# One-core block pair in f32: T by transposes, the last product with tokens on partitions, gathered modulation planned behind the norm, half-wide attention results in the last layer

## The chip, the cores and the metric

The kernel runs on one NeuronCore of a Trainium2 chip. The time is the device time of one execution in microseconds (us). Engines are written as in the profile: PE (TensorE matmul), PEld (TensorE weight load), DVE (VectorE), ACT (ScalarE), POOL (GpSimd), SP (SyncE, which issues all DMAs here).

## The reference

Two blocks in sequence on 256 tokens of width D = 1024, in f32. The first block has two layers, each of them a gated FFN, an attention mix and a second gated FFN; the second block has three mixers (RWKV-7, latent attention, differential attention), a gated merge, and an FFN with a short convolution. Cut to what the change touches:

```python
# first block, per layer l; x and a context of 256 tokens, each with its own modulation
mod = silu(c) @ w_ada[l] + b_ada[l]            # 9 vectors of width D: shift, scale, gate, three times
h = h + 0.5 * g1 * swiglu(modulate(rms_norm(h, norm_ffn1[l]), sh1, sc1), w_gate, w_up, w_down)   # FF = 2816
h = h + gm * (concat(y_w, y_g, y_n) @ w_out[l])         # attention; the context too, except in the last layer
h = h + 0.5 * g2 * swiglu(modulate(rms_norm(h, norm_ffn2[l]), sh2, sc2), ...)

# second block: the state of RWKV-7, token by token
sa = einsum('bhij,bhj->bhi', state, -kk_t)
state = state * w_t + sa[..., None] * b_t + v_t[..., None] * k_t

# its last product, and the final norm
u = conv3(rmsnorm(x, norm_ffn) @ w_up) + conv_b
x = x + (silu(gate) * val) @ w_down            # [256, 2816] @ [2816, 1024]
return rmsnorm(x, norm_final)
```

## The kernel before

**Precision.** An f32 product is made of three fp32r matmuls: each operand is split into a high and a low part (hi·hi, hi·lo, lo·hi). Every weight tile arrives by DMA in one of three slots "w"; ACT casts the high part to a "page" and DVE subtracts it from the tile for the low part (`TENSOR_TENSOR page<-w,page`). Activations lie with features on partitions and tokens along the row: 256 columns, or 512 where the context goes along.

**The order of the work.** Every operation is recorded first (`Plan`), and a list scheduler of the kernel's own then sets one fixed order per engine under limits on memory; `nc.after(i, j)` makes operation i wait for operation j in that planning. All instructions are issued from one line, L740 (L741 in the changed kernel). Memory is cut into pages of 2048 words per partition, a "small" area, three weight slots "w" and eight PSUM "banks"; one page can hold several tiles.

**Modulation.** `ada_steps(l, m)` gathers the modulation vector m of layer l: w_ada comes in row blocks `araw` of 128x1024, and each is multiplied by a column of silu(c) and added to `aacc`, for the tokens and for the context (r). That is 14 DVE operations of 128x1024 and two ACT copies for each m. They are recorded as "fill" steps between the tiles of the FFNs by `pop_fill`. Layer 0's m = 0 and 1 are made in another way (`first_mod`), inside the first FFN's first product: for each of eight k, DVE makes the modulation of 128 features (`mod0`, `G00`), scales the input and splits it, and PE then runs 12 matmuls 128x512 on it.

**T.** `rwkv_chunks` treats RWKV-7 in chunks of 128 tokens. For each of four (q, tb), with four heads in one 128x512 tile, the inverse of a triangular matrix is built level by level: W from X (eight matmuls that write 128x128, four of them pairs), a masked copy Wt by DVE, then

```python
pz = Wt^T Z ; px = Z^T Wt ; X -= px ; Z -= pz        # four 128x128 f32 matmuls each, one DVE 128x512 each
```

X is the transpose of Z throughout. Of five levels the last makes only Z, so px is made in 16 levels in all. The two tb of a q run interleaved.

**The last product.** `conv_ffn` loops over eight output blocks o; each takes two weight tiles of 1408 columns (`w2_dn`) and 22 x 3 matmuls 128x256 into one bank, DVE adds the result to the residual `hx`, and `norm_add` squares it for the sum over features. After the last block PE sums and broadcasts the norm, DVE scales eight blocks (`fin`), and eight DMAs of 128 KB write the result.

## Time and profile before

| what | value |
|---|---|
| time, median of 3 runs | 2346.76 us (2346.3 to 2348.51) |
| profiled execution | 2345.4 us, span 2343.5 us |
| mean granted TensorE clock | 0.990 of full speed |
| instructions | 35351 |
| busy share of the span | PE 98%, PEld 85%, DVE 70%, ACT 43%, POOL 2% |
| DMA | 328.20 MB, mean 140 GB/s |

The span runs from the first to the last instruction, and the 1.9 us between it and the execution's own time lie around it. PE is nearly always busy, so a microsecond that leaves PE's own work, or a stall of PE, is what can show in the time; work of DVE or ACT shows only where PE waits for it.

### The profile page before, as it was taken

The page shows a single profiled execution, that of the slowest core. Times are in us where ns is not written, and L with a number is a line of the kernel's source. Part 1 is how long each engine was busy: PE and PEld are TensorE (multiplying, and loading weights), DVE is VectorE, ACT ScalarE, POOL GpSimd, SP SyncE. Part 2 cuts the span into 40 slices and gives each one's busy share as a digit, 9 for nine tenths or more (in the row PEclk, how much of TensorE's full clock was granted, in tenths as well). Part 3 has the DMA queues.
Part 4 walks back from the last instruction along what each step waited for, and adds up shares of the span by engine and source line. Part 5 has one row for each costly group of instructions (what it writes and reads, how often), then busy time and mean ns, then how long its engine had stood idle before and what let it go on. Part 6 is the DMA issues. An engine that isn't in the chain of part 4 may idle for free. (4 is left out here: it accounts for less than half of the span.)

```text
span 2343.5 us, 35351 instructions
## 1 busy us (share of the span) xinstructions
PE 2288.6 (98%) x14170; PEld 2003.4 (85%) x14170; DVE 1632.0 (70%) x2860; ACT 1005.9 (43%) x1785; POOL 52.8 (2%) x66
## 2 busy tenths in 40 slices
PE   7999999999999999999999999999999999999998
PEld 5777788978787788788878888789999998999998
DVE  6948763795779999995333348776567767658874
ACT  3422322585543233233222236665456224646653
POOL 0000000010000000000000000000000010000000
PEclk9999999999999999999999999999999999999999
DMA  8636633203136775223132232234544111454543
GB/s 345 229 115 219 236 109 116 82 28 119 62 126 232 243 276 174 83 103 135 51 125 103 68 106 98 86 104 173 197 162 172 42 55 46 153 180 162 198 163 126
DMA packets 63106, 328.20 MB, mean 140 GB/s; under 512 B 8029, under 2 KB 11101, under 8 KB 40030
## 3 DMA queue, kind: packets, MB, share of 16 engines
q1 hardware_dynamic: 62942, 325.95, 39.3%
q8 instruction: 111, 1.82, 0.3%
q14 instruction: 53, 0.43, 0.1%
HBM read 324.87 MB, written 1.05 MB: 139 GB/s over the span
## 5 line engine op out<-in xcount | busy, mean ns | idle before, releaser
L740 PE MATMUL bank<-page,page 128*128 128x256 f32 (+8 forms) x12548 | 2163.4, 334 | 22.4 <-ACT page L740 14.6
L740 PEld LDWEIGHTS bank<-page,page 128*128 128x128 f32 (+3 forms) x12548 | 1846.6, 189 | 277.4 <-ACT page L740 34.8
L740 ACT CAST page<-w 128x1024 fp32r<-128x1024 f32 (+2 forms) x511 | 489.4, 962 | 898.3 <-PE bank L740 866.5
L740 DVE TENSOR_TENSOR page<-w,page 128x1024 fp32r<-128x1024 f32 (+2 forms) x511 | 566.3, 1112 | 375.6 <-ACT page L740 255.6
L740 DVE SCALAR_TENSOR_TENSOR page<-page,page,page 128x1024 f32<-128x1024 f32 x200 | 247.1, 1277 | 1.0 <-ACT page L740 1.0
L740 DVE TENSOR_TENSOR page<-page,bank 128x512 f32<-128x512 f32 (+2 forms) x168 | 93.7, 574 | 135.5 <-PE bank L740 132.9
L740 DVE SCALAR_TENSOR_TENSOR page<-bank,small,page 128x256 f32<-128x256 f32 (+2 forms) x240 | 111.4, 483 | 58.3 <-PE bank L740 55.4
L740 PE MATMUL bank<-page 128*128 128x256 f32 (+7 forms) x650 | 151.8, 308 | 0.0
L740 ACT ACTIVATE page<-bank,small 128x256 f32<-128x256 f32 (+2 forms) x216 | 115.3, 546 | 35.8 <-DVE small L740 25.8
L740 PE MATMUL bank<-small,page 128*128 128x128 f32 (+2 forms) x776 | 110.8, 270 | 19.4 <-DVE page L740 14.2
L740 PEld LDWEIGHTS bank<-small,page 128*128 128x128 f32 x776 | 95.3, 164 | 36.5 <-issue 13.1
L740 DVE TENSOR_TENSOR page<-page,page 128x256 fp32r<-128x256 f32 (+4 forms) x227 | 111.9, 507 | 12.7 <-ACT page L740 11.8
L740 ACT COPY page<-bank 128x512 f32<-128x512 f32 (+3 forms) x175 | 80.8, 496 | 85.2 <-PE bank L740 79.7
L740 ACT CAST page<-page 128x256 fp32r<-128x256 f32 (+1 forms) x165 | 78.0, 484 | 91.5 <-DVE page L740 89.3
L740 ACT ACTIVATE page<-bank 128x512 f32<-128x512 f32 (+3 forms) x163 | 81.7, 508 | 72.7 <-PE bank L740 72.0
L740 PEld LDWEIGHTS bank<-page 128*128 128x128 f32 (+2 forms) x650 | 105.1, 189 | 6.0 <-issue 0.7
L740 ACT ACTIVATE page<-page 128x256 f32<-128x256 f32 (+4 forms) x182 | 80.0, 454 | 57.9 <-DVE page L740 50.9
L740 ACT ACTIVATE page<-page,small 128x256 fp32r<-128x256 f32 (+1 forms) x124 | 56.9, 506 | 52.6 <-DVE page L740 26.0
L740 POOL TENSOR_TENSOR small<-small 128x2 f32<-128x2 f32 (+2 forms) x32 | 38.6, 1207 | 1793.5 <-DVE small L740 1453.1
L740 DVE TENSOR_TENSOR page<-bank,page 128x256 f32<-128x256 f32 (+2 forms) x109 | 51.6, 497 | 34.8 <-ACT page L740 19.7
L740 DVE TENSOR_REDUCE small<-bank 128x1 f32<-128x512 f32 (+3 forms) x132 | 67.3, 527 | 7.1 <-PE bank L740 6.8
L740 DVE COPY_PREDICATED page<-page,small 128x384 f32<-128x384 uint32 x124 | 66.2, 592 | 0.8
(51 smaller groups left out, 580.1 us busy)
## 6 DMA issues: line engine op xcount, KB each, us to landing
w<-in_gu_dram SPq DMA_DIRECT2D x88, 1024.0 KB, 4.8
page<-in_w_ada_dram SPq DMA_DIRECT2D x128, 512.0 KB, 4.6
w<-in_dn_dram SPq DMA_DIRECT2D x64, 704.0 KB, 4.0
w<-in_w_up_dram SPq DMA_DIRECT2D x22, 1024.0 KB, 4.8
w<-in_w_qk_dram SPq DMA_DIRECT2D x12, 1024.0 KB, 4.9
w<-in_w_gate_dram SPq DMA_DIRECT2D x12, 1024.0 KB, 4.8
w<-in_w_dn_dram SPq DMA_DIRECT2D x16, 704.0 KB, 4.0
page<-in_w_ada_dram SPq DMA_DIRECT2D x8, 1024.0 KB, 15.1
```

The source lines that it names most:

```text
L740: getattr(getattr(self.real, eng), m_)(*a_, **k_)
```

## The change

Four edits.

1. **T by transposes.** px and `X -= px` go. Z is updated first, and X is made from it by four PE transposes into one bank and one ACT copy 128x512 (`transposed`), in each of the 16 levels.
2. **The last product with tokens on partitions.** H is the stationary operand now (128 tokens) and the weights move, 512 columns at a time: 22 f x 2 tb x 2 column halves x 3 matmuls 128x512 into four banks that are held throughout; eleven weight tiles of 2048 columns. The residual is transposed beforehand (16 PE transposes, four ACT copies). The final norm is per partition: DVE add, ACT square with a row sum, DVE, POOL power, DVE scale by `gain_out`, and four output DMAs of 256 KB.
3. **Gathered modulation planned behind the norm.** The planner's mark, which was set by each `pop_fill`, is set once in `ffn`: behind the first product (first FFN of layer 0) or behind the norm. Layer 0's m = 2 and layer 1's m = 0 wait for it.
4. **y half wide.** The attention results of the last layer take 256 columns in place of 512 (there is no context there), which frees memory.

```diff
@@ pop_fill / ada_steps / ffn @@
         if self.fill:
-            self.mark = len(self.nc.ops) - 1
             self.fill.pop(0)()
...
-                        if l and m == 0:
+                        if m == (0 if l else 2):
                             nc.after(i, self.mark)
...
+            u_end = len(nc.ops) - 1
             for j in range(ahead):
                 glu(j, first[j], both[0])
-                self.pop_fill()
...
             u = self.norm(l, i_n, halves, rb if one else None)
+        self.mark = u_end if raws else len(nc.ops) - 1
...
-        y = [self.blk(f"y{j}") for j in range(KB)]
+        y = [self.blk(f"y{j}", S if last else T2) for j in range(KB)]
@@ rwkv_chunks @@
+        def transposed(z, x):
+            ps = hv(self.aux_ps("XT"))
+            with nc.run():
+                for hl in range(4):
+                    nc.tensor.transpose(ps[:, hl], z[:, hl], self.ident)
+            nc.scalar.copy(x, ps)
...
+                nc.vector.tensor_tensor(Z, Z, pz, op=OP.subtract)
                 if lv < 4:
-                    px = hv(self.aux_ps("px"))
-                    for hl in range(4):
-                        nc.tensor.matmul(px[:, hl], Z[:, hl], W[:, hl], start=True, stop=True)
-                    nc.vector.tensor_tensor(X, X, px, op=OP.subtract)
-                nc.vector.tensor_tensor(Z, Z, pz, op=OP.subtract)
+                    transposed(Z, X)
@@ conv_ffn @@
-        for o in range(KB):
-            ps = self.mm_ps("pdn")[:, :S]
-            for half in range(2):
-                w = self.wtile(a["w2_dn"][2 * o + half])
-                self.dense(ps, w, 0, H[HFB * half:], nk=HFB, first=half == 0, last=half == 1)
-            nc.vector.tensor_tensor(self.hx[:, o], self.hx[:, o], ps, op=OP.add)
-            self.norm_add(0, o)
-        rb = self.norm_rb(0)
-        for k in range(KB):
-            t = self.t256("fin")
-            nc.vector.scalar_tensor_tensor(t, self.hx[:, k], col[:, 74 + k:75 + k], rb, op0=OP.mult, op1=OP.mult)
-            nc.sync.dma_start(self.out[:, k], t)
+        gain = self.load("gain_out", [D])
...
+        pss = [[self.aux_ps("pdn") for _ in range(2)] for _ in range(2)]
+        def down(f, w, tb):
+            for c in range(2):
+                self.mm3n(pss[tb][c], w, D * (f % 2) + 512 * c, 512, H[f], slice(P * tb, P * tb + P),
+                          f == 0, f == NFB - 1)
...
+        for tb in range(2):
+            st = self.t("fst", [4])
+            for c in range(2):
+                x = xt[tb][:, 512 * c:512 * c + 512]
+                nc.vector.tensor_tensor(x, x, pss[tb][c], op=OP.add)
+                sq = self.t("fsq", [512])
+                nc.scalar.activation(sq, x, AF.Square, scale=1.0 / 32, accum_out=st[:, c:c + 1])
+            nc.vector.tensor_scalar(st[:, 2:3], st[:, 0:1], st[:, 1:2], EPS, op0=OP.add, op1=OP.add)
+            nc.gpsimd.tensor_tensor(st[:, 3:4], st[:, 2:3], self.mhalf[:, :1], op=OP.pow)
+            for c in range(2):
+                cs = slice(512 * c, 512 * c + 512)
+                o = self.t("fin", [512])
+                nc.vector.scalar_tensor_tensor(o, xt[tb][:, cs], st[:, 3:4], gain[:, cs], op0=OP.mult, op1=OP.mult)
+                nc.sync.dma_start(self.out[P * tb:P * tb + P, cs], o)
```

The planner sets the order anew, so instructions move on every engine. Three places follow.

**DVE in the first FFN's first product, near its end.** `SCALAR_TENSOR_TENSOR page,page,page 128x1024` are the accumulations of layer 0's m = 2; the 128x2 rows are modulation and `G00`, `TENSOR_SCALAR 128x256` scales the input, and the `TENSOR_TENSOR 128x256` after it is its low part, for which PE waits. Before:

```order
L740 SCALAR_TENSOR_TENSOR small<-small 128x2
L740 SCALAR_TENSOR_TENSOR page_106<-page_128,page_75,page_106 128x1024
L740 TENSOR_SCALAR page_75<-page_75,small 128x256
L740 SCALAR_TENSOR_TENSOR page_106<-page_128,page_75,page_106 128x1024
L740 TENSOR_TENSOR page_363<-page_75,page_363 128x256
L740 TENSOR_TENSOR page_363<-page_88,page_363 128x256
L740 TENSOR_TENSOR small<-bank_73,small 128x2
L740 SCALAR_TENSOR_TENSOR page_106<-page_135,page_75,page_106 128x1024
L740 TENSOR_TENSOR small<-bank_73,small 128x2
L740 SCALAR_TENSOR_TENSOR page_106<-page_135,page_75,page_106 128x1024
L740 SCALAR_TENSOR_TENSOR small<-small 128x2
L740 SCALAR_TENSOR_TENSOR page_106<-page_135,page_75,page_106 128x1024
```

And now, from the same instruction on:

```order
L741 SCALAR_TENSOR_TENSOR small<-small 128x2
L741 TENSOR_SCALAR page_75<-page_75,small 128x256
L741 TENSOR_TENSOR page_363<-page_75,page_363 128x256
L741 TENSOR_TENSOR page_363<-page_88,page_363 128x256
L741 TENSOR_TENSOR small<-bank_73,small 128x2 x2
L741 SCALAR_TENSOR_TENSOR small<-small 128x2
L741 TENSOR_SCALAR page_75<-page_75,small 128x256
L741 TENSOR_TENSOR small<-bank_67,small 128x2 x2
L741 TENSOR_TENSOR page_420<-page_75,page_420 128x256
L741 TENSOR_TENSOR page_420<-page_88,page_420 128x256
```

The accumulations have left this stretch; the first now stands 18 rows further on, behind the last split of the input and the low parts of the next weight tile.

**PE in the first half of T.** The rows 128x128 x4 with two pages are pz or px (before), the pairs x2 are W. Rows `bank<-small,page 128x128 x4` are four transposes (the identity lies in "small"). 128x256 rows are products of the mixers' input, which fill between. Before, one level of one chunk and the next of the other:

```order
L740 MATMUL bank_70<-page_10668,page_13579 128x128 x4
L740 MATMUL bank_73<-page_13579,page_10668 128x128 x4
L740 MATMUL bank_72<-page_13526,page_13636 128x128 x4
L740 MATMUL bank_71<-page_13636,page_13526 128x128 x3
L740 MATMUL bank_73<-page_13526,page_10668 128x128 x2
L740 MATMUL bank_73<-page_13526,page_1454 128x128 x2
```

And now:

```order
L741 MATMUL bank_68<-page_13566,page_13523 128x128 x2
L741 MATMUL bank_70<-small,page_13523 128x128 x4
L741 MATMUL bank_68<-page_13566,page_75 128x128 x2
L741 MATMUL bank_74<-page_420,page_3700 128x256
L741 MATMUL bank_74<-page_420 128x256 x2
L741 MATMUL bank_74<-page_420,page_761 128x256
L741 MATMUL bank_74<-page_3700,page_420 128x256
L741 MATMUL bank_73<-page_13523,page_6078 128x128 x2
L741 MATMUL bank_73<-page_13523,page_1441 128x128 x2
L741 MATMUL bank_71<-page_13566,page_13634 128x128 x4
```

In place of two products in a row stands pz alone (the last row), and the transposes of the other chunk stand later, between two pairs of its sibling's W, with 128x256 products behind them.

**DVE behind the last matmul.** Before, the add of the last output block, the norm's epsilon, and the eight scales:

```order
L740 TENSOR_TENSOR page_81<-page_81,bank_70 128x256
L740 TENSOR_SCALAR small<-bank_71 128x2
L740 SCALAR_TENSOR_TENSOR page_75<-page_81,small,bank_74 128x256 x8
```

And now, from the first of the four adds on:

```order
L741 TENSOR_TENSOR page_75<-page_75,bank_73 128x512
L741 TENSOR_TENSOR page_75<-page_75,bank_68 128x512
L741 TENSOR_SCALAR small<-small 128x1
L741 TENSOR_TENSOR page_75<-page_75,bank_71 128x512
L741 TENSOR_TENSOR page_75<-page_75,bank_69 128x512
L741 SCALAR_TENSOR_TENSOR page_10571<-page_75,small,page_10571 128x512
L741 SCALAR_TENSOR_TENSOR page_13401<-page_75,small,page_10571 128x512
L741 TENSOR_SCALAR small<-small 128x1
L741 SCALAR_TENSOR_TENSOR page_10571<-page_75,small,page_10571 128x512
L741 SCALAR_TENSOR_TENSOR page_75<-page_75,small,page_10571 128x512
```

The first 128 tokens (banks 73 and 68) are added first, and their two scales stand between the adds of the second 128 tokens and that half's epsilon. On PE the last twelve matmuls write banks 71 and 69 alone.

## Rows read from the trace of the kernel before

**Rows 1.** The page's first part: busy us, share of the span, instructions.

```profile
PE 2288.6 (98%) x14170; PEld 2003.4 (85%) x14170; DVE 1632.0 (70%) x2860; ACT 1005.9 (43%) x1785; POOL 52.8 (2%) x66
```

**Rows 2.** Windows: length, busy of PE, PEld, DVE, ACT, POOL; clock, DMA, GB/s.

```profile
1100.00:1150.00 50.00, 50.00 (x222) 41.43 (x221) 14.31 (x18) 13.23 (x17) 0.00 (x0) 1.00 0.18 64
...
2050.00:2100.00 50.00, 50.00 (x419) 50.00 (x418) 27.88 (x29) 22.09 (x31) 0.00 (x0) 1.00 0.53 184
```

**Rows 3.** Windows of the two stretches in which T runs.

```profile
1827.00:1875.00 48.00, 48.00 (x412) 45.71 (x411) 34.22 (x63) 9.69 (x18) 0.00 (x0) 1.00 0.09 28
1905.00:1952.00 47.00, 47.00 (x402) 44.48 (x401) 32.98 (x66) 8.59 (x20) 3.19 (x3) 1.00 0.13 46
```

**Rows 4.** Timeline of PE in T: start, length, operation, count.

```profile
1847.41 1.17 PE L740 MATMUL bank<-page,page 128*128 128x128 f32 x9
...
1831.72 0.60 PE L740 MATMUL bank<-small,page 128*128 128x128 f32 x4
```

**Rows 5.** Groups by form: busy us, mean ns of one, idle before, its releaser.

```profile
L740 DVE TENSOR_TENSOR page<-page,bank 128x512 f32<-128x512 f32 x98 | 65.6, 685 | 100.3 <-PE bank L740 99.6
...
L740 ACT COPY page<-bank 128x512 f32<-128x512 f32 x89 | 48.8, 590 | 30.6 <-PE bank L740 25.8 <-DVE small L740 4.5
L740 DVE SCALAR_TENSOR_TENSOR page<-page,small,bank 128x256 f32<-128x256 f32 x103 | 43.4, 475 | 8.3 <-PE bank L740 8.3
...
L740 ACT ACTIVATION_READ_ACCUMULATOR page<-bank,small 128x1 f32 x128 | 26.5, 207 | 0.0
...
L740 DVE SCALAR_TENSOR_TENSOR page<-page,page,page 128x1024 f32<-128x1024 f32 x200 | 247.1, 1277 | 1.0 <-ACT page L740 1.0
```

**Rows 6.** DMA issues: KB each, median us from issue to landing.

```profile
w<-in_w_up_dram SPq DMA_DIRECT2D x22, 1024.0 KB, 4.8
...
out_dram<-page SPq DMA_DIRECT2D x8, 128.0 KB, 2.0
```

**Rows 7.** Timeline from the last block's add to the last output's issue.

```profile
2332.88 0.42 DVE L740 TENSOR_TENSOR page<-page,bank 128x256 f32<-128x256 f32 x1 [6.12 <-PE bank L740]
2333.40 0.42 ACT L740 ACTIVATE page<-page 128x256 f32<-128x256 f32 x1 [7.50 <-DVE page L740]
...
2335.04 0.70 POOL L740 TENSOR_TENSOR small<-small 128x2 f32<-128x2 f32 x1 [191.06 <-DVE small L740]
...
2336.54 3.22 DVE L740 SCALAR_TENSOR_TENSOR page<-page,small,bank 128x256 f32<-128x256 f32 x8 [1.58 <-PE bank L740]
2337.09 3.79 SPq L740 DMA_DIRECT2D out_dram<-page  x8
```

**Rows 8.** Timeline of PE near the end of the first product.

```profile
54.56 4.72 PE L740 MATMUL bank<-page,page 128*128 128x512 f32 x13 [2.15 <-ACT page L740]
```

**Rows 9.** Timeline of DVE in the same stretch.

```profile
46.49 1.28 DVE L740 SCALAR_TENSOR_TENSOR page<-page,page,page 128x1024 f32<-128x1024 f32 x1
...
53.67 0.40 DVE L740 TENSOR_SCALAR page<-page,small 128x256 f32<-128x256 f32 x1
...
54.40 1.27 DVE L740 SCALAR_TENSOR_TENSOR page<-page,page,page 128x1024 f32<-128x1024 f32 x1
```

**Rows 10.** Window behind that wait of PE.

```profile
54.56:57.77 3.21, 3.21 (x8) 2.49 (x9) 2.63 (x7) 1.20 (x3) 0.00 (x0) 0.50 0.10 42
```

**Rows 11.** Windows of the first FFN behind its first product.

```profile
62.00:100.00 38.00, 37.73 (x171) 29.81 (x170) 37.28 (x41) 15.57 (x21) 3.13 (x6) 1.00 0.69 235
100.00:150.00 50.00, 50.00 (x227) 40.49 (x226) 37.82 (x38) 15.18 (x19) 0.00 (x0) 1.00 0.56 187
150.00:200.00 50.00, 47.97 (x215) 38.07 (x214) 27.20 (x36) 13.13 (x17) 0.00 (x0) 1.00 0.33 115
```

**Rows 12.** Window from layer 0's second to layer 1's first FFN.

```profile
661.00:690.00 29.00, 29.00 (x203) 27.21 (x202) 19.30 (x31) 13.74 (x24) 0.00 (x0) 1.00 0.29 110
```

**Rows 13.** Window of layer 0's attention.

```profile
426.00:651.00 225.00, 222.72 (x1351) 185.28 (x1349) 167.37 (x434) 140.36 (x340) 7.36 (x4) 1.00 0.19 69
```

**Rows 14.** Group by form in that attention: transposes.

```profile
L740 PE MATMUL bank<-small,page 128*128 128x128 f32 x216 | 29.7, 275 | 0.5 <-DVE small L740 0.5
```

More of the change, by code (lines that the diff above doesn't have):

```diff
@@ L182, in layout2 @@
     a["w2_up"] = np.ascontiguousarray(np.stack([up[:NFB], up[NFB:]], 2)).reshape(NFB, P, -1)
-    b = f["ffn_w_down_2"][0].reshape(2, HFB, P, KB, P).transpose(3, 0, 2, 1, 4)
-    a["w2_dn"] = np.ascontiguousarray(b).reshape(2 * KB, P, HFB * P)
+    a["w2_dn"] = np.ascontiguousarray(
+        f["ffn_w_down_2"][0].reshape(HFB, 2, P, D).transpose(0, 2, 1, 3)).reshape(HFB, P, 2 * D)
+    a["gain_out"] = np.ascontiguousarray(np.broadcast_to(f["norm_final_2"].reshape(1, D), (P, D)))
     mu = f["rwkv_mu_2"][0][order]
@@ L190, in layout2 @@
             _pcol(f["b_gate_2"][0]), _pcol(f["diff_subln_2"][0]), _pcol(f["norm_mix_2"][0]),
-            _pcol(f["norm_ffn_2"][0]), _pcol(f["norm_final_2"])]
+            _pcol(f["norm_ffn_2"][0])]
     a["col2"] = np.ascontiguousarray(np.concatenate(cols, 1))
@@ L1449, in setup2 @@
         nc = self.nc
-        self.col = self.load("col2", [82])
+        self.col = self.load("col2", [74])
         self.conv = self.load("conv2", [4, 44])
@@ L1715, in rwkv_chunks @@
             nc.vector.tensor_tensor(Z, idb, Z, op=OP.subtract)
-            ps = hv(self.aux_ps("XT"))
-            for hl in range(4):
-                nc.tensor.transpose(ps[:, hl], Z[:, hl], self.ident)
-            nc.scalar.copy(X, ps)
+            transposed(Z, X)
             for lv in range(5):
@@ L1728, in rwkv_chunks @@
                     nc.tensor.matmul(pz[:, hl], W[:, hl], Z[:, hl], start=True, stop=True)
+                nc.vector.tensor_tensor(Z, Z, pz, op=OP.subtract)
                 if lv < 4:
-                    px = hv(self.aux_ps("px"))
-                    for hl in range(4):
-                        nc.tensor.matmul(px[:, hl], Z[:, hl], W[:, hl], start=True, stop=True)
-                    nc.vector.tensor_tensor(X, X, px, op=OP.subtract)
-                nc.vector.tensor_tensor(Z, Z, pz, op=OP.subtract)
+                    transposed(Z, X)
             ps = self.aux_ps("MV")
@@ L1922, in conv_ffn @@
             H.append(Hv)
-        self.acc = {}
-        for o in range(KB):
-            ps = self.mm_ps("pdn")[:, :S]
-            for half in range(2):
-                w = self.wtile(a["w2_dn"][2 * o + half])
-                self.dense(ps, w, 0, H[HFB * half:], nk=HFB, first=half == 0, last=half == 1)
-            nc.vector.tensor_tensor(self.hx[:, o], self.hx[:, o], ps, op=OP.add)
-            self.norm_add(0, o)
-        rb = self.norm_rb(0)
-        for k in range(KB):
-            t = self.t256("fin")
-            nc.vector.scalar_tensor_tensor(t, self.hx[:, k], col[:, 74 + k:75 + k], rb, op0=OP.mult, op1=OP.mult)
-            nc.sync.dma_start(self.out[:, k], t)
+        gain = self.load("gain_out", [D])
@@ new lines, in conv_ffn @@
+        xt = [self.t(f"xt{tb}", [D]) for tb in range(2)]
+        for tb in range(2):
+            for c in range(2):
+                ps = self.aux_ps("hT")
+                with nc.run():
+                    for k in range(4):
+                        nc.tensor.transpose(ps[:, P * k:P * k + P], self.hx[:, 4 * c + k, P * tb:P * tb + P], self.ident)
+                nc.scalar.copy(xt[tb][:, 512 * c:512 * c + 512], ps)
+        pss = [[self.aux_ps("pdn") for _ in range(2)] for _ in range(2)]
[3 more added lines that the diff above has]
+                          f == 0, f == NFB - 1)
@@ new lines, in conv_ffn @@
+        for f in range(0, NFB, 2):
+            w = self.wtile(a["w2_dn"][f // 2])
+            fs = (f, f + 1)
+            for g, tb in [(g, tb) for g in fs for tb in range(2)] if f < NFB - 2 else [(g, tb) for tb in range(2) for g in fs]:
+                down(g, w, tb)
+        for tb in range(2):
+            st = self.t("fst", [4])
[6 more added lines that the diff above has]
+            nc.gpsimd.tensor_tensor(st[:, 3:4], st[:, 2:3], self.mhalf[:, :1], op=OP.pow)
+            for c in range(2):
+                cs = slice(512 * c, 512 * c + 512)
+                o = self.t("fin", [512])
+                nc.vector.scalar_tensor_tensor(o, xt[tb][:, cs], st[:, 3:4], gain[:, cs], op0=OP.mult, op1=OP.mult)
+                nc.sync.dma_start(self.out[P * tb:P * tb + P, cs], o)
@@ L2186 @@
         aps[name] = nc.dram_tensor(f"in_{name}_dram", a.shape, mybir.dt.from_np(a.dtype), kind="ExternalInput").ap()
-    out = nc.dram_tensor("out_0_dram", (P, KB, S), F32, kind="ExternalOutput").ap()
+    out = nc.dram_tensor("out_0_dram", (S, D), F32, kind="ExternalOutput").ap()
     with _tile.TileContext(nc) as tc:
@@ L2191 @@
     got = r.results[0]["out_0_dram"]
-    return np.ascontiguousarray(got.transpose(1, 0, 2).reshape(D, S).T)[None]
+    return np.ascontiguousarray(got)[None]
```

## The prediction

> **What bounds it now.** I read first the busy shares, then the windows of 50 us to find where PE is not full, then the timeline at those places. PE is busy 98% of the span, DVE 70%, ACT 43% [rows 1]. So the reader is to ask of each edit one of two things: does it take work from PE itself, or does it end a wait of PE? In the dense products PE is full to the last: 222 matmuls 128x512 in 50 us are 0.225 us each, and 419 matmuls 128x256 are 0.119 each [rows 2]. In the two stretches of T it is just as full, 48.00 of 48.00 and 47.00 of 47.00, while DVE has a quarter and ACT four fifths of the time free [rows 3]. What is left are waits at three sorts of places: the start, the attention layers, and the tail behind the last matmul.
>
> **T.** A level loses px: four f32 matmuls 128x128, which the trace shows as two records each. Nine records took 1.17 us; with the last one's own length (0.28, the group mean of such records [rows 14]) taken off, eight steps of 0.111 [rows 4]. So px is 8 x 0.111 = 0.89. Four transposes took 0.60, three steps of 0.11 [rows 4], so 0.44. A level gains 0.45, and 16 levels gain **7.2 us**, since PE is full there. DVE loses 16 times 0.685 and ACT gets 16 times 0.590 [rows 5], 9.4 us more in two stretches of 95 us in which it now works 18 [rows 3]: hidden.
>
> What could take it back is the chain. Before, a level ran W 0.89, mask 0.69, pz 0.89, px 0.89, X's subtraction 0.69: 4.05 us. Now it runs W, mask, pz, Z's subtraction, transposes 0.44, copy 0.59: 4.19, with six crossings between engines in place of four; a crossing took 0.10 from DVE's add to ACT's square [rows 7], and I take 0.2. That makes 5.4. The two chunks that run side by side had 2 x 2.67 = 5.3 us of PE work a level, which covered the old chain (4.85); they now have 4.4, so each pair of levels needs about 1 us of other products. The order shows such products between the steps of the first half, and fewer in the second. If all eight pairs went without, T would cost 8 x 1 and come out at +0.8; bounds -7.2 and +0.8. I take -7.2: the row it is nearest to is that of a full PE.
>
> **The last product.** Out go 528 matmuls of 256 columns, 528 x 0.119 = 62.8; in come 264 of 512, 264 x 0.225 = 59.4 [rows 2]: **-3.4 us**. The 16 transposes of the residual cost 16 x 0.11 = **+1.8**; their four copies (0.59 each) and the cast work, the same number of weight columns as before, lie on ACT and DVE, which have 28 and 22 us free in 50 beside the products of 256 columns [rows 2]. The bounds are -5 (a 512-column matmul at 2 x 0.111) and 0.
>
> Here a rule speaks against the rows. The Trainium skill ("TensorE: Matmul & The Clock Gate", section "Back-to-back issue gap") gives an isolated matmul 262 cycles at 256 columns and 518 at 512. By that, an estimate from that page at 2.4 GHz, the two products would be 57.6 and 57.0 us and the edit worth 0.6 rather than 3.4. The rows show the 256-column matmul dearer than that by a tenth, with the weight load busy 50.00 of 50.00 beside it, and the rows decide.
>
> **The tail.** From the last block's add at 2332.88 [rows 7] to the end of the span at 2343.5 it is 10.6 us. Afterwards, counted from the last matmul: the add of the first column half began 0.68 before (three matmuls of 0.225) and ends at 0.06; the second add ends at 0.75 (0.685 each [rows 5]); ACT's square (0.59, as a copy of that size) and its accumulator read (0.21 [rows 5]) end at 1.65 after a crossing of 0.1; DVE has by then begun the two scales of the first 128 tokens, each 0.74 (between 0.475 at 256 columns and 1.277 at 1024 [rows 5]), and is free at 2.23; epsilon 2.4; POOL's power 0.70 [rows 7], 3.15; two scales, 3.94 and 4.68. Before, 3.74 us passed from DVE's last scale (2336.54 + 3.22) to the end, of which 0.65 went by before the eighth of the issues at 0.47 each could begin [rows 7]. Four issues 0.74 apart don't queue. A 256 KB transfer lands later than the 2.0 us of 128 KB; between that and 4.8 for 1024 KB [rows 6], 2.4. So 4.68 + 3.74 - 0.65 + 0.4 = 8.2: **-2.4 us**, with bounds -1.5 (power and squares of both halves in a row) and -3.4 (no wait for the first half's scales, transfers no slower).
>
> **The start.** DVE runs six accumulations of 1.28 us between 46.49 and 55.67 [rows 9], in front of the modulation, scale and split that PE's first product is to have next. PE waits 2.15 us, up to 54.56 [rows 8]; then it works 3.21 us at clock 0.50, the lower of its two levels [rows 10], after which it is at 1.00 again [rows 11]. In the changed order none of the six stands there. Five of them, 6.4 us, were ahead of the scale at 53.67 [rows 9], so more than the 2.15 is freed; and without the wait before it I expect no fall of the clock: 2.15 + 3.21 / 2 = **-3.8 us**. Bounds 0 (the splits wait for something else just behind) and -5.
>
> The accumulations must go somewhere. From 62 to 100 us DVE is busy 37.28 of 38.00, then 37.82 and 27.20 of 50 [rows 11]. Moved by six or eight (8 to 10 us) they fill the 12 free us of 100 to 150; the queue of SP now issues the next weight tile ahead of four w_ada loads, not behind them. I price this at 0, with a bound of +6: half of the moved 10 us in front of low parts of weights that PE waits for, plus half a clock piece or so.
>
> **The rest.** Layer 1's m = 0 moves ahead of the first tiles of its FFN, where DVE has 29 - 19.3 = 9.7 us free [rows 12] and the changed order puts six accumulations, 7.7 us, ahead of the first low part: hidden, 0. The half-wide y only frees memory, and the planner orders everything behind anew: 0, within 4 us either way, about what three waits like that of rows 8 come to with their clock.
>
> **Sum.** -7.2 - 3.4 + 1.8 - 2.4 - 3.8 = -15.0. The profiled execution took 2345.4 us (span 2343.5 and 1.9 around it), so 2330.4; it lies 1.4 below the median 2346.76, against which the forecast is **2331.8 us**, its own range 2326 to 2337. A measurement of this kernel can tell about 0.2%, 4.7 us, from no change.
>
> **Rivals.**
> - *T's chain shows.* Against the full windows of [rows 3] stands that the pair's own PE work falls below the chain. At 1 us in six to eight pairs it takes back 6 to 8 us: 2338 to 2340. Chance 0.14.
> - *The start's gain is given back.* DVE is nearly full up to 100 us [rows 11], so the moved accumulations meet weight splits there. +4 to +8: 2336 to 2340. Chance 0.12.
> - *More waits go than I count*, in the attention layers (in layer 0 PE stood still for 225 - 222.72 = 2.3 us [rows 13]), by the new order: 2316 to 2326. Chance 0.10.
> - *The clock falls in T: slower.* PE's full clock would have to depend on what kind of work it does, and transposes replace products. If the two stretches, 47 + 48 - 7 = 88 us, ran at clock 0.50, each us would take two: 2331.8 + 88 = 2420. It decides from nine pieces like that of [rows 10] at 1.6 us each, which use up the 15.0; from thirteen the kernel is slower by over 0.2%. Against it: layer 0's attention ran 225 us at clock 1.00 [rows 13] with 216 transposes [rows 14], 216 x 0.11 = 24 us, a tenth of the time; in T it will be 40 in 44 us, again a tenth. Chance 0.04. The Trainium skill ("TensorE: Matmul & The Clock Gate", Part 4, on the PE-mode transpose) states that the full clock doesn't engage for transposes, as they don't count as busy in the same way; by that rule this rival would be likelier than the row lets me think.
> - *Nothing comes of it*: the DVE waits of layer 1 start (14 x 1.28 = 17.9 us against 9.7 free, all ahead of the low parts, 8 us) on top of one of the first two: 2343 to 2348. Chance 0.05.
>
> **Numbers.** The forecast's range has 0.55. The range from 2320 to 2342 adds both give-backs and half of the better case, 0.55 + 0.26 + 0.06 = 0.87, and leaves out less than the 2 in 10 that may be left out; cutting it at 2339 would cut into both give-backs at once. Faster by over 0.2% is below 2342.1: 0.55 + 0.14 + 0.12 + 0.10 less 0.04 for give-backs that come together or run past their price = 0.87. Slower (above 2351.5): the clock's 0.04 and 0.02 of unseen reordering, 0.06. The rest, 0.07, is the same.
>
> **What would show it.** T: the two stretches together 7 us shorter, PE full, clock 1.00, transposes in steps of 0.11; wrong if PE shows waits with ACT as releaser behind the copies. Last product: matmuls in steps of 0.225. Tail: about 8.2 us behind the last matmul. Start: no PE wait over 1 us between 46 and 62 us and no clock of 0.50 at 54. Give-back: PE waits for DVE between 62 and 150 us. The forecast is wrong by more than its range if the planner's new order opens a wait of several us in an attention layer, which no row here can rule out.

## The result, and the profile after

The changed kernel takes 2321.22 us (median of 4 runs, 2319.57 to 2323.79) against 2346.78 us before (4 runs): ratio 0.9891, 95% interval 0.9879 to 0.9904, so 25.6 us less (22.5 to 28.4). The forecast was 2331.8 us with a range of 2320 to 2342. The time lies in that range, but below the forecast's own 2326 to 2337: the gain is 1.7 times the 15.0 us that were summed.

The profiled execution took 2319.57 us, the fastest of the four, with a span of 2317.8 us. First the page's first part, as [rows 1], and the line of the core's span and mean granted clock:

```profile
PE 2271.4 (98%) x13846; PEld 1981.9 (86%) x13846; DVE 1618.8 (70%) x2821; ACT 1013.3 (44%) x1795; POOL 54.0 (2%) x67
...
core 0: 2317.8 us, clock 0.995
```

PE's busy time fell by 17.2 us and the rest of the 25.7 us of span was waiting. The clock says something that the busy shares hide, since a busy PE at half clock counts as busy: its mean was 0.990 of full speed before and 0.995 now. What these lack of 1 is 23.4 us of 2343.5 and 11.6 of 2317.8, but the two can't simply be subtracted. The changed trace has no record of a low clock at its start, and yet five matmuls 128x512 took 2.28 us there, up to the next at 30.57, which is 0.46 each and twice the 0.225 of a dense product:

```profile
28.29 2.48 PE L741 MATMUL bank<-page,page 128*128 128x512 f32 x5
...
28.00:32.00 4.00, 4.00 (x12) 3.23 (x12) 3.48 (x11) 3.26 (x6) 0.00 (x0) 1.00 1.02 420
```

Behind the start the falls can be counted. From 54 us to the last matmul the clock fell to 0.50 ten times before (at 54, 423, 652 twice, 1037, 1409, 1471, 1887 twice, 1973 us) and five times now (416, 648, 1030, 1402, 1556). A fall costs up to 1.7 us, so at most 8.5 us of clock came back there. In the other three runs of the changed kernel the mean clock was 0.993 to 0.994, so the profiled one lost the least.

Where did the time go? The same instruction can be followed through both traces at places where PE waits for the same thing. Timeline rows of PE, before and then after; the bracket is the idle time ahead of the row and what ended it:

```profile
420.57 0.71 PE L740 MATMUL bank<-small 128*128 128x128 f32 x4 [0.67 <-POOL small L740]
...
1787.31 0.39 PE L740 MATMUL bank<-page,page 128*128 128x256 f32 x1 [0.63 <-ACT page L740]
...
1971.37 0.92 PE L740 MATMUL bank<-page,page 96*128 96x128 f32 x4 [2.56 <-ACT page L740]
...
2019.60 1.58 PE L740 MATMUL bank<-page,page 128*128 128x256 f32 x11 [1.13 <-ACT page L740]
```

```profile
56.02 1.19 PE L741 MATMUL bank<-page,page 128*128 128x512 f32 x4 [1.30 <-ACT page L741]
...
414.72 0.71 PE L741 MATMUL bank<-small 128*128 128x128 f32 x4 [0.67 <-POOL small L741]
...
1780.50 0.38 PE L741 MATMUL bank<-page,page 128*128 128x256 f32 x1 [0.62 <-ACT page L741]
...
1953.20 0.55 PE L741 MATMUL bank<-small,page 128*128 128x128 f32 x3 [1.81 <-ACT page L741]
...
1999.37 1.33 PE L741 MATMUL bank<-page,page 128*128 128x256 f32 x9 [1.14 <-ACT page L741]
```

| place | before | after | difference so far | in this stretch |
|---|---|---|---|---|
| last wait of the first product [rows 8] | 54.56 | 56.02 | +1.5 | +1.5 |
| norm ahead of layer 0's attention | 420.57 | 414.72 | -5.9 | -7.3 |
| second block's first projections | 1787.31 | 1780.50 | -6.8 | -1.0 |
| branch products, behind RWKV-7 and the two other mixers | 2019.60 | 1999.37 | -20.2 | -13.4 |
| end of the span | 2343.5 | 2317.8 | -25.7 | -5.5 |

The +1.5 at the start is no edit's: a kernel with the start ordered as before (run e5_only_T below) had the same wait end at 55.91 us, and one with the start of the changed kernel (e1_no_T) had it end at 54.51. Three stretches carry the gain. The forecast's 3.8 for the start lies in the first two rows, where 5.9 stand together; it had 7.2 where 13.4 stand, and 4.0 where 5.5 stand.

The first FFN, windows as [rows 11] (length, busy of PE, PEld, DVE, ACT, POOL, then clock, DMA, GB/s), the last of 200 to 250 us, which before had PE busy 48.66:

```profile
100.00:150.00 50.00, 50.00 (x227) 40.45 (x226) 44.77 (x45) 16.60 (x21) 0.00 (x0) 1.00 0.56 190
150.00:200.00 50.00, 50.00 (x231) 39.54 (x230) 25.52 (x37) 12.61 (x16) 0.00 (x0) 1.00 0.35 119
200.00:250.00 50.00, 50.00 (x226) 40.45 (x226) 44.50 (x49) 16.37 (x19) 0.00 (x0) 1.00 0.85 325
```

PE has no wait left from 150 to 250 us, where it had 2.0 and 1.3, and the moved accumulations show as DVE's 44.77 in place of 37.82. The two stretches of T, as [rows 3], and the last product, as [rows 2]:

```profile
1822.00:1868.00 46.00, 46.00 (x399) 43.90 (x398) 28.57 (x50) 14.32 (x26) 0.00 (x0) 1.00 0.08 30
1890.00:1936.00 46.00, 45.99 (x390) 43.28 (x386) 34.27 (x70) 18.16 (x37) 3.12 (x3) 1.00 0.20 69
...
2260.00:2310.00 50.00, 50.00 (x222) 41.43 (x221) 21.27 (x20) 17.27 (x19) 0.24 (x1) 1.00 0.35 123
```

T is full and at full clock, and ACT has the copies (14.32 and 18.16 us busy, 9.69 and 8.59 before). Behind each half of T the clock had fallen, and in this execution it doesn't (in that of e8_product_256, whose order is the same up to the last product, it does once). The window of before behind the second half, and the two of after behind the first and the second:

```profile
1960.00:1976.00 16.00, 13.38 (x81) 11.11 (x80) 14.09 (x48) 6.97 (x19) 1.11 (x1) 0.90 0.01 2
```

```profile
1866.00:1880.00 14.00, 14.00 (x112) 12.29 (x112) 9.18 (x26) 6.59 (x17) 3.00 (x2) 1.00 0.20 77
1940.00:1956.00 16.00, 13.93 (x94) 11.22 (x94) 13.90 (x53) 8.16 (x27) 2.09 (x2) 1.00 0.00 1
```

The end, as [rows 7]:

```profile
2310.08 0.39 PE L741 MATMUL bank<-page,page 128*128 128x512 f32 x1
2310.60 0.63 ACT L741 ACTIVATE page<-page 128x512 f32<-128x512 f32 x1 [1.24 <-DVE page L741]
2311.11 1.41 DVE L741 SCALAR_TENSOR_TENSOR page<-page,small,page 128x512 f32<-128x512 f32 x2
...
2312.77 0.55 POOL L741 TENSOR_TENSOR small<-small 128x1 f32<-128x1 f32 x1 [2.46 <-issue]
2313.36 1.41 DVE L741 SCALAR_TENSOR_TENSOR page<-page,small,page 128x512 f32<-128x512 f32 x2 [0.72 <-POOL small L741]
```

From the last matmul's end at 2310.47 to 2317.8 it is 7.3 us, where 10.6 were before. The two scales of the first 128 tokens stand in DVE between the adds and the last epsilon, as the order said.

### The profile page after: what moved, and what is told of

It reads as the page before. It is cut to its first block, busy times and chain, and to the rows that moved or that the text cites. A ratio compares the mean times of both kernels' runs of the same rounds, so it can differ in the third digit from the quotient of the medians.

```text
span 2317.8 us, 34646 instructions
## 1 busy us (share of the span) xinstructions
PE 2271.4 (98%) x13846; PEld 1981.9 (86%) x13846; DVE 1618.8 (70%) x2821; ACT 1013.3 (44%) x1795; POOL 54.0 (2%) x67
## 5 line engine op out<-in xcount | busy, mean ns | idle before, releaser
L741 PE MATMUL bank<-page,page 128*128 128x256 f32 (+7 forms) x12178 | 2138.7, 337 | 15.1 <-ACT page L741 9.9
L741 PEld LDWEIGHTS bank<-page,page 128*128 128x128 f32 (+4 forms) x12178 | 1814.5, 188 | 270.2 <-ACT page L741 24.9
L741 DVE SCALAR_TENSOR_TENSOR page<-page,page,page 128x1024 f32<-128x1024 f32 x212 | 262.1, 1278 | 2.3 <-ACT page L741 1.4
L741 DVE TENSOR_TENSOR page<-page,bank 128x512 f32<-128x512 f32 (+2 forms) x148 | 83.6, 574 | 112.5 <-PE bank L741 103.2
L741 PE MATMUL bank<-small,page 128*128 128x128 f32 (+2 forms) x848 | 121.3, 270 | 18.7 <-DVE page L741 13.3
L741 DVE TENSOR_TENSOR page<-page,page 128x256 fp32r<-128x256 f32 (+4 forms) x265 | 127.4, 497 | 12.9 <-ACT page L741 12.0
L741 ACT COPY page<-bank 128x512 f32<-128x512 f32 (+3 forms) x195 | 92.4, 504 | 95.5 <-PE bank L741 91.0
L741 PEld LDWEIGHTS bank<-small,page 128*128 128x128 f32 x848 | 103.4, 162 | 35.3 <-issue 13.0
L741 PEld LDWEIGHTS bank<-page 128*128 128x128 f32 (+2 forms) x628 | 105.2, 189 | 10.6 <-ACT page L741 3.1
L741 ACT ACTIVATE page<-page 128x256 f32<-128x256 f32 (+5 forms) x178 | 79.8, 460 | 63.1 <-DVE page L741 56.4
L741 POOL TENSOR_TENSOR small<-small 128x2 f32<-128x2 f32 (+3 forms) x33 | 39.9, 1211 | 1781.3 <-DVE small L741 1771.1
## 6 DMA issues: line engine op xcount, KB each, us to landing
page<-in_w_ada_dram SPq DMA_DIRECT2D x8, 1024.0 KB, 15.1
```

The source lines that it names most:

```text
L741: getattr(getattr(self.real, eng), m_)(*a_, **k_)
```

## The experiments

Theory 1: each edit is worth the work and the waits that it takes from PE, and nothing else. Theory 2: the new order also moved or ended falls of TensorE's clock, which come where PE does small products, and these are the rest of the gain. The runs show where the clock fell; what makes it fall they don't show.

T is the first edit, P the last product with its norm, M the gathered modulation's mark, Y the half-wide y. Times are medians; each ratio is to runs of the kernel before that were taken beside it.

| run | kernel | us | ratio, 95% interval | against its before |
|---|---|---|---|---|
| e1_no_T | changed, T undone | 2331.19 | 0.9935, 0.9922 to 0.9947 | -15.1 |
| e2_no_product | changed, P undone | 2327.72 | 0.9922, 0.9909 to 0.9934 | -18.5 |
| e3_no_mark | changed, M undone | 2331.13 | 0.9931, 0.9917 to 0.9945 | -15.1 |
| e4_no_half_y | changed, Y undone | 2324.53 | 0.9906, 0.9893 to 0.9920 | -21.7 |
| e5_only_T | before with T | 2336.40 | 0.9958, 0.9946 to 0.9971 | -10.4 |
| e6_only_mark | before with M | 2340.79 | 0.9968, 0.9956 to 0.9981 | -6.0 |
| e7_only_half_y | before with Y | 2344.63 | 0.9991, 0.9982 to 1.0000 | -2.2 |
| e8_product_256 | changed, product in 256 columns | 2324.75 | 0.9907, 0.9893 to 0.9920 | -22.0 |
| e9_before_wide | before, 16 wide matmuls more | 2344.21 | 0.9987, 0.9978 to 0.9995 | -2.6 |
| e10_norm_fill_1 | changed, fillers in the norms | 2318.45 | 0.9880, 0.9867 to 0.9894 | -28.3 |
| e11_norm_fill_3 | changed, three times as many | 2317.92 | 0.9876, 0.9861 to 0.9891 | -28.8 |
| e12_only_product | before with P | 2338.12 | 0.9962, 0.9949 to 0.9976 | -9.0 |

**One edit undone (e1 to e4).** Each takes the lines of one edit back to those of before:

```diff
# e1_no_T
-                    transposed(Z, X)
+                    px = hv(self.aux_ps("px"))
...
+                    nc.vector.tensor_tensor(X, X, px, op=OP.subtract)
# e2_no_product: the loop over o, norm_rb and eight outputs again
# e3_no_mark
+            self.mark = len(self.nc.ops) - 1
-                        if m == (0 if l else 2):
+                        if l and m == 0:
...
+                self.pop_fill()
-        self.mark = u_end if raws else len(nc.ops) - 1
# e4_no_half_y
-        y = [self.blk(f"y{j}", S if last else T2) for j in range(KB)]
+        y = [self.blk(f"y{j}") for j in range(KB)]
```

> The changed kernel with T as before (px by matmuls), the other three edits kept. Theory 1 (each edit is worth the work and waits it takes from PE, and nothing else): T is worth 16 x 0.45 = 7.2 us, so 2321.2 + 7.2 = 2328.4. Theory 2 (the new order also took away falls of the clock, three of which stood in the T stretches of before at 1888 and 1973 us, 1.7 us each): T's order brings these back, 2328.4 + 5.1 = 2333.5, and the windows behind the first T stretch show a clock of 0.50 again.

> The changed kernel with the last product and the final norm as before, the other three edits kept. Theory 1: the product gave 3.5 us, the tail 3.3 (10.6 to 7.3 us behind the last matmul), the transposes of the residual cost 1.75, so 2321.2 + 5.0 = 2326.2. Theory 2: the edit stands last in the program, so nothing ahead of it is ordered anew, and it says the same; a time beyond 2328 would mean that the order ahead moved too.

> The changed kernel with the gathered modulation planned as before, the other three edits kept. Theory 1: the start's wait and its fall of the clock (3.8 us) come back, and so do the waits at 189 and 223 us (2.1 + 1.1) and their like, together about 6 us by the curve of the two traces from 60 to 250 us: 2321.2 + 9 = 2330. Rival: the waits at 189 and 223 went by accident of the new order, and only the start's 3.8 come back: 2325.

> The changed kernel with the last layer's y 512 columns wide again, the other three edits kept. Theory 1: y's width takes no work from PE, so 2321.2. Theory 2: the freed memory moves the order from layer 1's attention on (1400 us and later), and with it where the clock falls: up to three falls, 1.7 us each, 2321 to 2326.

Against the changed kernel's 2321.22 they cost 10.0, 6.5, 9.9 and 3.3 us, 29.7 together and 4.1 more than all four gave. P and Y cost 1.5 and 3.3 more than theory 1 has for them. With M undone PE's waits of 150 to 250 us are back, at 47.93 and 48.66 of 50, and so is the start's (2.13 us); that these waits went by accident falls with it. The start's fall of the clock isn't back: the clock is 1.00 from 50 to 62 us. So theory 1 has M's sum right, by parts that are not quite those it names.

**One edit alone (e5, e6, e7, e12).** The same lines, put into the kernel before.

> The kernel before with T by transposes alone. Theory 1 (work alone): 2346.5 - 7.2 = 2339.3. Theory 2 (the order moves the clock too): the 14 us of narrow work behind the first T stretch, after which the clock of before fell for 6.8 us, is shorter in the new order, and one or two falls of 1.7 us go as well: 2336 to 2338. Rival of step 1: the chain of six crossings shows and T alone gives less than 4 us, 2343 or more.

> The kernel before with the gathered modulation planned behind the norm, alone. Theory 1: the wait and the fall of the clock near 54 us and the waits at 189 and 223 us go, about 9 to 10 us, and nothing behind 300 us changes by it: 2346.5 - 9.5 = 2337. Rival: the gain hangs on the other edits, and alone it is the 3.8 us of the start: 2342.7.

> The kernel before with y half wide in the last layer, alone: not one instruction of PE goes. Theory 1: 2346.5, no change. Theory 2 (the freed memory orders layer 1's attention anew): its waits of 1.6 and 1.1 us at 1467 to 1470 and the fall of the clock at 1471 go, about 3.3 us as in the run without it: 2343.

> The kernel before with the last product and the final norm of the changed kernel, alone. Theory 1: 3.5 us of product and 3.3 of tail, less 1.75 for the transposes of the residual: 2346.7 - 5.0 = 2341.7. Theory 2: nothing ahead of the last product is ordered anew but the loads of constants, so the falls of the clock stay as in before: the same. If the edits only add up, the four alone (10.4, 6.0, 2.2 and this) should come to the 25.6 of all: 7.0, 2339.7.

T alone gives 10.4: the chain of crossings doesn't show. P alone gives 9.0, 4.0 more than its work, and Y alone 2.2 without taking an instruction from PE (at the edge of what 11 runs tell from nothing). The four come to 27.5, the whole to 25.6. One place shows how that can be: the stretch behind the first half of T, before, and in e7 and e12 (windows as above, one fence for each kernel; under e7's and e12's the timeline row of the head sums in that stretch):

```profile
1880.00:1895.00 15.00, 15.00 (x90) 13.26 (x91) 9.30 (x26) 5.74 (x14) 2.63 (x2) 0.77 0.20 72
```

```profile
1880.00:1895.00 15.00, 15.00 (x115) 13.20 (x115) 11.56 (x31) 5.82 (x15) 3.00 (x2) 1.00 0.21 71
...
1885.53 2.11 PE L740 MATMUL bank<-small,page 128*128 128x2 f32 x17
```

```profile
1880.00:1895.00 15.00, 15.00 (x115) 13.08 (x114) 11.44 (x31) 5.70 (x15) 2.98 (x2) 1.00 0.21 72
...
1885.65 2.12 PE L741 MATMUL bank<-small,page 128*128 128x2 f32 x17
```

PE is busy throughout in all three and runs the same instructions in the same order here. In the kernel before it runs them at a mean clock of 0.77, so it loses 0.23 x 15 = 3.4 us, two falls to 0.50 of 1.7 us each; in the other two it loses nothing. The head sums began at 1884.24 before (the row is shown at e9) and 1.3 and 1.4 us later in those two; in e6, with the same order again, they began at 1880.31 and the clock was 0.77. Whether it falls there thus hangs on something that a small change ahead moves, and no run shows what. In the traces of P alone and of Y alone both falls are gone, in that of T alone one of them, and they can go only once.

What is an edit's own, and what is the clock's, comes apart when a stretch between two waits that all kernels have is compared in all traces of kernels without added matmuls. For T it is the one from the first projections to the branch products; its two ends in e1 and in e5, and the window behind the second half of T in the changed kernel and in e8:

```profile
1780.08 1.56 PE L741 MATMUL bank<-page,page 128*128 128x256 f32 x8 [0.63 <-ACT page L741]
...
2008.99 2.29 PE L741 MATMUL bank<-page,page 128*128 128x256 f32 x17 [1.17 <-ACT page L741]
```

```profile
1788.80 2.28 PE L740 MATMUL bank<-page,page 128*128 128x256 f32 x14 [0.63 <-ACT page L740]
...
2010.81 1.45 PE L740 MATMUL bank<-page,page 128*128 128x256 f32 x10 [1.14 <-ACT page L740]
```

```profile
1945.00:1985.00 40.00, 37.93 (x324) 35.12 (x320) 28.45 (x85) 21.82 (x59) 1.05 (x1) 1.00 0.33 117
```

```profile
1945.00:1985.00 40.00, 37.93 (x310) 35.20 (x307) 28.27 (x85) 21.43 (x57) 1.05 (x1) 0.96 0.31 106
```

The falls are counted by the clock of two windows: from 1870 to 1900 us 0.94 is one fall and 0.89 two, from 1945 to 1985 us 0.96 is one.

| kernel | stretch of T, us | falls in it | less 1.7 us for each |
|---|---|---|---|
| before | 232.29 | 3 | 227.2 |
| e6, before with M | 232.28 | 3 | 227.2 |
| e7, before with Y | 228.83 | 1 | 227.1 |
| e12, before with P | 228.87 | 1 | 227.2 |
| e1, changed without T | 228.91 | 1 | 227.2 |
| changed | 218.87 | 0 | 218.9 |
| e2, without P | 220.44 | 1 | 218.7 |
| e3, without M | 220.40 | 1 | 218.7 |
| e4, without Y | 221.99 | 2 | 218.6 |
| e5, before with T | 222.01 | 2 | 218.6 |
| e8, product in 256 columns | 220.41 | 1 | 218.7 |

T is worth 8.4 us here whatever stands beside it. The falls come and go, and of the six traces with T only that of the changed kernel has none. The other stretches read the same way. From the start's wait to the norm ahead of layer 0's attention, without a fall of the clock, it is 358.7 us in the changed kernel, e1, e2 and e8, which have M, and 365.1 in e3, which hasn't. With one fall it is 360.4 in e4 and e6, which have M, and 366.0 in the kernel before, e5 and e7, and 366.7 in e12, which haven't. So M's own part there is 5.6 to 6.4 us. The two ends in e3:

```profile
57.98 1.20 PE L741 MATMUL bank<-page,page 128*128 128x512 f32 x4 [2.13 <-ACT page L741]
...
423.09 0.71 PE L741 MATMUL bank<-small 128*128 128x128 f32 x4 [0.67 <-POOL small L741]
```

From the branch products to the end it is 323.8 to 324.2 us in the five kernels without P (the one before, e2, e5, e6 and e7) and 318.4 to 318.5 in five with it (the changed one, e1, e3, e4 and e12): 5.5 for P. Y shortens no stretch. What e7 gained is the two falls behind the first half of T. Of the five falls that e4 has more than the changed kernel, three, at 57, 416 and 648 us, stand ahead of 1330 us, from where on its order differs, so y's width can't have made them. So 8.4 + 5.6 + 5.5 = 19.5 of the 25.7 us of span are the edits' own. One fall behind the start's wait and three in T's stretch are 6.8, the third row of the table of places has 1.0, and 1.5 was lost at the start; with rounding that is the whole.

M alone gives 6.0 where it costs 9.9 when undone. Its trace shows the waits of 150 to 250 us gone (50.00 and 50.00), but a clock of 0.65 from 56 to 60 us behind the start's wait, and the changed kernel's 1.00 there:

```profile
55.88 2.25 PE L740 MATMUL bank<-page,page 128*128 128x512 f32 x7 [1.30 <-ACT page L740]
...
56.00:60.00 4.00, 4.00 (x12) 3.18 (x13) 1.56 (x5) 1.20 (x3) 0.00 (x0) 0.65 0.00 0
```

The wait itself is 1.30 us in both, so M shortened it by 0.85, and the clock decides over 1.4 more here. Its five runs spread from 2333.82 to 2341.19; what made the one fast run isn't known.

**The product's price (e8).** Same layout, weights, transposes and tail, only the matmuls cut in two:

```diff
-            for c in range(2):
-                self.mm3n(pss[tb][c], w, D * (f % 2) + 512 * c, 512, H[f], ...)
+            for c in range(4):
+                self.mm3n(pss[tb][c // 2][:, S * (c % 2):S * (c % 2) + S], w, D * (f % 2) + S * c, S, H[f], ...)
```

> The changed kernel with each of the last product's 512-column matmuls cut into two of 256 columns, the same weights, transposes and tail. By the rows (0.119 to 0.120 against 0.225 to 0.227 us) 528 x 0.1195 = 63.1 in place of 264 x 0.2265 = 59.8: 2321.2 + 3.3 = 2324.5. By a matmul whose time is its columns and a small fixed cost, +0.6: 2321.8. If the whole 6.8 us of this stretch came from the wider matmul, +6: 2327.

It took 3.5 us more than the changed kernel, and its window shows why; PEld is the second figure:

```profile
2262.00:2312.00 50.00, 50.00 (x419) 50.00 (x419) 19.56 (x17) 15.71 (x15) 0.00 (x0) 1.00 0.35 122
```

A matmul of 256 columns takes 0.119 us in this layout as in the old one, with the weight load busy all the time; of 512 columns 50 / 222 = 0.225, with the load busy 41.43 of 50. The rows' price holds. The price of an isolated matmul that the Trainium skill gives ("TensorE: Matmul & The Clock Gate", section "Back-to-back issue gap"), by which the two products would have differed by 0.6 us, doesn't hold for this stream.

**Work added, time taken off (e9).** Is it the kind of work that lets the clock fall? PE's rows of the kernel before in that stretch:

```profile
1882.45 1.31 PE L740 MATMUL bank<-page 128*64 128x128 f32 x5
...
1884.24 2.11 PE L740 MATMUL bank<-small,page 128*128 128x2 f32 x17
...
1886.63 2.66 PE L740 MATMUL bank<-page,page 128*128 128x64 f32 x15
```

Products that write 2, 64 and 128 columns follow each other without a gap, with a few of 256 columns among them (two rows of 128x256 x2 between 1886 and 1892 us). The edit puts 256-column products between, into free halves of the same banks; nothing reads them:

```diff
+        def wide(ps, j, n=4):
+            for k in range(n):
+                i = nc.tensor.matmul(ps[:, S:], u[k][:, 0, :P], u[k][:, 0, :S], start=True, stop=True)
+                nc.after(i, j)
...
+            if q:
+                wide(ps, len(nc.ops) - 1)      # ahead of two head sums and two broadcasts
```

> The kernel before with 16 matmuls of 256 columns more, whose results nobody reads (1.9 us of added work on PE), four each ahead of the two head sums and the two broadcasts of the second half's preparation: in the stretch of 1880 to 1894 us, where PE was busy throughout, but with products that write 2, 64 and 128 columns, and where the clock fell to 0.50 for 6.8 us. The planner's order is otherwise as before up to there. Theory 2 (the clock falls on this narrow work and not on the share of busy time): the clock stays at 1.00 there, -3.4 + 1.9, so 2346.5 - 1.5 = 2345.0, and no 0.50 between 1880 and 1900 in the profile. Rival (the fall comes from elsewhere, or by the position in time): 0.50 stays there and the time is 2346.5 + 1.9 = 2348.4.

```profile
1883.00:1898.00 15.00, 15.00 (x118) 13.37 (x117) 11.16 (x31) 5.79 (x14) 3.00 (x2) 1.00 0.22 72
```

The clock stays at 1.00, and the kernel with 1.9 us more work takes 2.6 us less. That agrees with theory 2 and doesn't show it. e7 and e12 show that a small shift in time does the same, and the head sums began 3.8 us later here (at 1888.01). Nor is the time the clock's alone: the order was not "as before up to there" but another from about 1588 us on, and most of the wait in the latent attention is gone too. PE was busy 37.38 of 40 us there before, and 39.21 in e9:

```profile
1945.00:1985.00 40.00, 37.38 (x283) 33.27 (x283) 32.30 (x100) 22.02 (x63) 2.15 (x2) 0.96 0.08 28
```

```profile
1945.00:1985.00 40.00, 39.21 (x301) 35.34 (x301) 34.27 (x103) 22.59 (x61) 5.18 (x5) 1.00 0.08 28
```

**Fillers in the norms (e10, e11).** In each norm of the first block PE does sums of one column, waits, and broadcasts. One or three f32 matmuls of 256 columns, read by nobody, go into the free half of the broadcast's bank:

```diff
         rb = self.aux_ps("nrb")
+        for _ in range(3):
+            nc.tensor.matmul(rb[:, S:], self.ident, self.hh(KB - 1, r), start=True, stop=True)
```

> The changed kernel with one f32 matmul of 256 columns more (two records of 0.21 us, read by nobody) ahead of each norm's broadcast, 12 in the six norms of the first block, where PE does matmuls of one column and waits. Theory 2: it breaks up stretches of 4.5 to 5 us in which the clock now falls once or twice each (at 416, 648, 1031 and 1403 us); if it is enough, four to six falls go, 1.7 us each, less at most 5 us of added work, most of it in waits: 2321 - 7 + 2 = 2316. If one is too little: 2321 to 2324, with 0.50 at the same places.

> As the run before, with three in place of one. Added work is 1.27 us for each half's norm, up to 15 us in all, of which the waits there hide 1 to 2 us a norm. Theory 2: no 0.50 at 416, 648, 1031 and 1403; the time 2321 - 8 + 7 = 2320. Rival (the falls come from the waits themselves, which the fillers don't end): the falls stay and the time is 2321 + 7 = 2328 or more.

Windows around two of these norms, of the changed kernel and then of e11:

```profile
412.00:420.00 8.00, 6.76 (x42) 6.11 (x41) 6.49 (x16) 3.78 (x8) 2.24 (x2) 0.79 0.43 180
643.00:652.00 9.00, 7.28 (x45) 6.87 (x45) 7.65 (x19) 3.54 (x9) 2.21 (x2) 0.81 0.34 117
```

```profile
404.00:416.00 12.00, 11.97 (x88) 11.11 (x88) 9.73 (x19) 6.29 (x11) 1.55 (x1) 1.00 0.38 131
638.00:648.00 10.00, 10.00 (x76) 9.63 (x75) 7.97 (x17) 4.34 (x9) 1.52 (x1) 1.00 0.28 105
```

With three fillers no fall is left at the four norms, and with one only that at 416 us. e11 is the fastest kernel here: its runs took 2316.29 to 2318.31 us, the changed kernel's 2319.57 to 2323.79 (four each, and the intervals of their ratios overlap). But the gain isn't where the falls went. In e11's trace the start's wait and the first projections stand at

```profile
52.06 5.29 PE L741 MATMUL bank<-page,page 128*128 128x512 f32 x22 [1.30 <-ACT page L741]
...
1776.95 2.04 PE L741 MATMUL bank<-page,page 128*128 128x256 f32 x12 [0.62 <-ACT page L741]
```

Between the two it takes 1724.9 us, the changed kernel 1724.5, and e10, with one filler, 1723.1. So the three fillers cost there what the falls and waits gave back, and e11's lead of 4.0 us in this trace comes ahead of 52 us: in the first norm the fillers wait for nothing but the input, and PE works from 7.06 us on in place of 10.78. The fillers end PE's idle time as well as its narrow work, so this pair doesn't tell those two apart as causes of the falls. The kernel before, whose clock fell between 1880 and 1895 us where PE never idled, shows that a fall needs no idle time.

## Why the prediction was right, and where it was too small

**The time** lies 1.2 us above the lower end of the range, and one of the four runs lies below it. The range reached down there for half of the better case, whose place was wrong. That the time was held is partly luck.

**T.** The work was sized rightly: four transposes take 0.60 us in the changed trace too, in steps of 0.11, the windows are full, and ACT's copies and the longer chain are hidden, so the term's -7.2 and not its other bound +0.8 came true. The stretch gave 13.4, of which 8.4 are T's own. What the term left out there is a shorter wait in the latent attention (PE idle for 2.07 of 16 us and not 2.62) and about 0.6 us that no row explains. The other 5.0 are three falls of the clock, two near 1888 us and one near 1973 us, which are not T's: five other traces of kernels with T have one or two of them.

**The clock rival** (0.04) had the wrong sign: the clock is 1.00 in both T stretches. The Trainium skill's rule on the PE-mode transpose ("TensorE: Matmul & The Clock Gate", Part 4), by which transposes don't count as busy in the same way, is not tested by this: they are about a tenth of the work here, and beside the products the clock held.

**The last product** was right: -3.4 forecast, 3.5 in e8 (its bound of -5 doesn't follow from the figure given: 264 x 0.222 is 58.6, which makes it -4.2). **The tail** gave 3.3 rather than 2.4: the power took 0.55 and not 0.70, and from the last scale's end (2313.36 + 1.41) to the end of the span passed 3.0 us, where the working had 3.5. **The half-wide y** was right at 0.

**The start** failed in part. "In the changed order none of the six stands there" is true, but "more than the 2.15 is freed" isn't: 1.30 us of wait stays. The bound's other case came, in which the splits wait for something else. DVE now idles there, waiting for PE's own modulation matmuls:

```profile
54.30 0.23 DVE L741 TENSOR_TENSOR small<-bank,small 128x2 f32<-128x2 f32 x2 [3.54 <-PE bank L741]
```

The clock's 1.6 came or didn't by the execution: e4 and e6 have M and the fall, e3 has neither.

**The step that failed** is "I price this at 0, with a bound of +6": the moved accumulations, which were worth -5.6 or more. They didn't delay weight splits; the moves took them out of the way of others. Before, three stood ahead of a weight's low part that PE needed at 189 us, and PE waited:

```profile
186.00 3.67 DVE L740 SCALAR_TENSOR_TENSOR page<-page,page,page 128x1024 f32<-128x1024 f32 x3
...
191.38 1.90 PE L740 MATMUL bank<-page,page 128*128 128x512 f32 x7 [1.96 <-DVE page L740]
```

e3 and e6 show that M alone ends this and the wait at 223 us, 3.4 us by the two windows of [rows 11] and 200 to 250 us. The rest of M's 5.6 to 6.4 us in the first FFN stands in no row as a wait. The trace of before held these waits, and the working looked for what the moved work would hit, not for what it had been hitting.

**The better case** (0.10) named its place wrongly: the waits that went were in the first FFN, not in layer 0's attention, and the rest was clock, which the working counted only behind a wait.

What stays open: what makes the clock fall, and why it falls in one execution and not in the next of the same order.

## What to carry to other kernels

When PE looks full, multiply the span by what the mean granted clock lacks of 1: that time is in no busy share, and here it was 23.4 us, more than any edit's work. It is a rough figure: falls over waits and behind the last matmul count in it, and a slow start may not. Before a gain is put down to an edit, count the falls in one stretch of several kernels: with 1.7 us taken off for each, eleven traces fell into two groups that agree within 0.3 us, and one trace alone would have given T 5 us too much. And when work is moved off a stretch, look in the trace for what it was standing in front of before asking what it will stand in front of next.

## What the hardware showed that was not expected

PE busy 15.00 of 15.00 us, for the most part with products of 2 to 128 columns, ran at a mean clock of 0.77, and the same matmuls in the same order a little over a microsecond later at 1.00. Adding 16 matmuls made that kernel 2.6 us faster, and adding 36 f32 matmuls in the norms made the changed one 3.3 us faster, by medians of runs whose spreads don't meet; in neither do the traces put the whole gain down to the clock.
